# A two-layer diffusion trunk on one NeuronCore: the second head of four pairs with queries on partitions, and an issue order planned in rounds

## The chip, the core and the metric

The kernel runs on one core of a Trainium2 chip. The metric is device time in microseconds, from launch to the last result. Before the change three runs took 1436.07 us in the median (1434.85 to 1436.29). Five engines work side by side, each through its own queue in order: PE (TensorE, matmuls; its weight loads are shown as PEld), DVE (VectorE), ACT (ScalarE), POOL (GpSimd) and SP, which here issues nearly all DMAs. They wait for each other by semaphores.

## The reference, cut to what matters

Two layers act on 1024 latent tokens and 256 context tokens of width 1024. Layer A is grouped attention (16 query heads, 4 key heads, 64 wide) with normed and rotated queries and keys; layer B is neighbourhood attention on a 16 by 64 grid. Both have a SiLU gate. The part that is changed is layer A's attention over 1280 keys:

```
k_all = jnp.concatenate([kc, k], axis=1)
v_all = jnp.concatenate([vc, v], axis=1)
def block(qi):
    s = jnp.einsum('bqkgd,bskd->bkgqs', qi, k_all).astype(jnp.float32) * ATTN_SCALE
    p = jax.nn.softmax(s, axis=-1).astype(v_all.dtype)
    return jnp.einsum('bkgqs,bskd->bqkgd', p, v_all)
o = lax.map(block, qb)
yx = (o * jax.nn.silu(z)) @ w_out
```

Each layer also needs modulation vectors, `silu(c) @ w_mod + b_mod`, for a scale, a shift and a gate. The last layer's stream is normed.

## The kernel before

Matmuls are in float16, with numbers held as a high part and a low part, so that a product of two such numbers is three matmuls (high by high, high by low, low by high). Tokens are in ten tiles of 128, eight latent (`NX`) and two of context (`NC`).

**The start** (`ln_pre`, `mod_cols`, `h_kt`, `kv_mm`, `kv_post`): tokens are normed, transposed on PE (`pl`), scaled by ACT with the modulation columns (`tf`) and split; these columns come from small matmuls (`pm`, then `pmc`), one block of 128 columns at a time. Key and value projections (`pkv`) of four tiles run along, eight blocks deep.

**Layer A's attention** goes by eight pairs of heads, `u` = 0 to 7. `a_proj(u)` projects queries and gate (`pa`, line 838), norms and rotates, and lays the queries out feature-first by a DMA transpose (line 855) as `q1`, with a copy of the low part in `q2` (line 857). `mgen` then finds each query's greatest score with matmuls of their own (`pm`, line 868, and `pmc`, line 874), which DVE reduces (lines 869 and 875); `rows` turns the maxima into a row of `q2` by four small matmuls (`pr`, line 907) and one ACT write (line 908), so that the score matmul subtracts them itself. `a_att(u, pt_)` works a block of 512 queries (`pt_` 0 and 1; 2 is the context block of 256), head `i` = 0 and then 1: for each of ten key tiles it makes the scores with keys on partitions (`st`, lines 987 and 988, two PSUM banks), ACT takes the exponential twice (`ph`, line 972, and `pf`, line 974), POOL, and DVE for every sixth tile, gets the low part `pl` (lines 929 and 926), and PE multiplies weights by values, three matmuls for each 128 queries (lines 935 to 937). A constant column of the values gives the row sums. `o_out` gates, splits and transposes the result into `o_hi` and `o_lo`, two tiles for the whole layer (tags Y0 and Y1).

**Layer B's attention** (`b_att`) has queries on partitions: DVE adds the bias while it takes the maximum (line 1250), ACT exponentiates with the maximum as bias and sums (lines 1268 to 1271), one DMA transposes both parts of the weights (line 1274), and PE uses two matmuls for each tile of keys (lines 1279 and 1281).

**What sets the order.** `timeline` interleaves the generators by hand-set times; this gives a program order. `Planner` then reads the whole program as a graph, gives each instruction a cost and a latency, and runs through it once: each engine takes, of the instructions that are ready, the first in program order. Small glued groups on PE come ahead. The order it finds is fixed by added dependencies (`apply`). Modulation weights of later use are loaded during layer A by `mod_block` in blocks of 1024 by 512 (`wg`, one buffer), which wait in SP's queue among the other loads.

Of the kernel before, what the change touches and what calls it, by code (L numbers as in the profile page):

```python
# [12 lines left out]
F32 = mybir.dt.float32  # L13
F16 = mybir.dt.float16
# [7 lines left out]
P = 128  # L22
D = 1024
# [12 lines left out]
GW, GR = 64, 16  # L36
BEV, BLAG = 2, 4
# [4 lines left out]
class Planner:  # L42
# [110 lines left out]
    def graph(self):  # L153
# [58 lines left out]

        self.glued = set()
# [32 lines left out]
    def schedule(self, key=None, margin=0.0, scale=None):  # L246
        scale = scale or {}
        N = len(self.node)
        key = key or (lambda i: -1 if i in self.glued else i)
# [11 lines left out]
        free = {k: list(v) for k, v in self.free.items()}  # L261
# [12 lines left out]
        def opened(i):  # L274

            r = 0.0
            for name in self.need.get(i, ()):
# [13 lines left out]
                r = max(r, min(free[k]))  # L291
# [15 lines left out]
        while count < N:  # L307
# [29 lines left out]
            for name in self.need.get(i, ()):  # L337
                ck = self.tiles[name][0].cap_key
                free[ck].remove(min(free[ck]))
                q[ck].popleft()  # L340
# [33 lines left out]
            for name in self.users[i]:  # L374
                left[name] -= 1
                end[name] = max(end[name], fin)
                if not left[name]:
                    tl, _, _, pool = self.tiles[name]
                    free[tl.cap_key].append(end[name])
# [16 lines left out]
        self.order, self.start, self.done = order, start, done  # L396
        return max(done)

# [31 lines left out]
def trunk_kernel(ctx, tc, x, cx, cc, norm_g, b_cols, sel_c, w_mod, b_mod, a_w_in, a_qg, a_kg, a_w_out,  # L430
# [24 lines left out]
    V.tensor_copy(id16, idf)  # L455
    mhalf = main.tile([P, 8], F32, name="mhalf")
# [7 lines left out]
    s2 = main.tile([P, KT, 32], F32, name="s2")  # L464
# [41 lines left out]
    def mod_block(pool, l, c0):  # L506

        nm = f"{l}{c0}"
        wm = pool.tile([P, KT, 512], F32, name="wg" + nm, tag="wg", bufs=1)
        r, k = c0 // D, slice(c0 % D // P, c0 % D // P + 4)  # L510
        for kt in range(KT):
            DM.dma_start(wm[:, kt], w_mod[l, kt * P:(kt + 1) * P, c0:c0 + 512])
            yield 1.0
        row = pool.tile([P, P], F32, name="mrow" + nm, tag="mrow", bufs=1)
        if r == 2:
            brow = com.tile([P, 512], F32, name="brow" + nm, tag="stage", bufs=4)[0:1]
            DM.dma_start(brow, b_mod[l:l + 1, c0:c0 + 512])
        ps = ps_pj(f"pmg{nm}", shape=(P, 2, P))
        for kt in range(KT):
            for j in range(4):  # L520
                T.matmul(ps[32 * j:32 * j + 32, 0], s2[:, kt, :], wm[:, kt, j * P:(j + 1) * P], start=kt == 0,
                         stop=r < 2 and kt == KT - 1)
        if r == 2:
            for j in range(4):
                T.matmul(ps[32 * j:32 * j + 32, 0], twos, brow[:, j * P:(j + 1) * P], start=False, stop=True)
            V.tensor_scalar_mul(row, ps[:, 0], 0.5 / WS)
            for v in range(2):
                DM.dma_start(gate_d[l, v, c0 - 2 * D:c0 - 2 * D + 512].rearrange("(j c) -> j c", c=P), row[v:P:32])
        else:
            V.tensor_copy(row, ps[:, 0])  # L530
# [63 lines left out]
    xstage = [main.tile([P, 4, D], F32, name=f"xstage{j}", tag=f"Y{j}") for j in range(2)]  # L594
# [862 lines left out]
```

## Time and profile before

| what | us |
|---|---|
| median of three runs | 1436.07 |
| the profiled execution, device time | 1435.4 |
| its span, first to last instruction | 1433.3 |
| PE busy in the span | 1369.1 |
| DVE busy | 970.2 |
| ACT busy | 933.1 |
| POOL busy | 637.5 |
| PE idle from 140 to 735 us (layer A's attention) | 2.6 |
| PE idle from 870 to 1330 us (layer B's attention) | 13.3 |

Busy means that at least one instruction of the engine ran; matmuls overlap, and a matmul's listed duration is longer than the distance to the next one. The profile's views name a group by line, engine, operation and tiles (result, arrow, sources). A wait is put down to the instruction whose semaphore came last. Granted TensorE clock over the span is 0.996 of full speed.

### The profile page before, as it was taken

What the parts mean: (1) busy time and instruction counts of PE and PEld (TensorE: products, weight loads), DVE (VectorE), ACT (ScalarE), POOL (GpSimd) and SP (SyncE); (2) the same over time, 40 slices, a digit from 0 to 9 for tenths busy, and PEclk for the clock granted to TensorE, in tenths of its full rate; (3) what the DMA queues carried; (4) which work ended last, traced back from release to release, by engine and by line L of the source; (5) the groups of instructions that cost most, each with busy time, mean ns of one, the idle gap of its engine ahead of it and who ended that gap; (6) DMA issues with size and microseconds to landing.
All of it is one profiled execution on the core that took longest, in us unless ns stands there. A gap on an engine that the chain in (4) does not pass through costs nothing.

```text
span 1433.3 us, 35760 instructions
## 1 busy us (share of the span) xinstructions
PE 1369.1 (96%) x13874; PEld 951.0 (66%) x13874; DVE 970.2 (68%) x2341; ACT 933.1 (65%) x2226; POOL 637.5 (44%) x871
## 2 busy tenths in 40 slices
PE   5799999999999999999999899999999999999797
PEld 2357777777777777776555476767677676767443
DVE  4697877777777777688234736686676757686833
ACT  3452778786868786788735626776676767776811
POOL 2321677766767676677852201312222222313432
PEclk9999999999999999999999999999999999999999
DMA  9753114143222213144123405575665757567932
GB/s 282 212 149 100 40 24 115 23 122 79 59 79 59 79 43 80 34 141 120 44 89 103 148 29 111 91 157 111 136 120 108 156 95 156 92 153 142 185 102 103
DMA packets 327410, 153.01 MB, mean 107 GB/s; under 512 B 234020, under 2 KB 306372, under 8 KB 327240
## 3 DMA queue, kind: packets, MB, share of 16 engines
q1 hardware_dynamic: 326664, 150.70, 43.5%
q8 instruction: 108, 1.77, 0.5%
q14 instruction: 62, 0.51, 0.1%
q10 hardware_dynamic: 576, 0.03, 0.0%
HBM read 85.65 MB, written 12.06 MB: 68 GB/s over the span
## 4 chain that ended last, share of the span: by engine, by line
PE 84%; DVE 9%; ACT 2%; DMA 2%; issue 2%; POOL 1%; SPq 0%; DVEq 0%; POOLq 0%; ACTq 0%
PE pa L838 13%; PE pb L1167 13%; PE pvz L1199 10%; PE poa L1080 7%; PE pob L1370 5%; PE st L987 5%; PE st L988 4%; PE pm L868 3%; PE pkv L734 3%; PE pv L936 3%; PE pv L937 3%; PE pv L935 3%; PE pvz L1202 1%; PE bpv L1279 1%; DVE bk L1185 1%
## 5 line engine op out<-in xcount | busy, mean ns | idle before, releaser
L929 POOL TENSOR_TENSOR pl<-pf,ph 128x256 f16<-128x256 f32 x544 | 368.6, 704 | 134.8 <-ACT pf L974 110.5
L972 ACT ACTIVATE ph<-st 128x512 f16<-128x512 f32 x320 | 192.4, 603 | 107.3 <-PE st L988 105.7
L929 POOL TENSOR_TENSOR bph<-bpf,bph 128x256 f16<-128x256 f32 (+1 forms) x128 | 98.0, 783 | 339.4 <-ACT bpf L1270 305.9
L838 PE MATMUL pa<-wa,x 128*128 128x256 f16 x1536 | 233.6, 272 | 1.3 <-DVE q16q L664 1.3
L869 DVE TENSOR_REDUCE mxp<-pm 128x1 f32<-128x512 f32 x256 | 170.6, 684 | 49.9 <-PE pm L868 48.2
L1167 PE MATMUL pb<-hb_hi,wb 128*128 128x512 f16 (+1 forms) x640 | 194.1, 359 | 3.2 <-DVE bk L1185 3.2
L974 ACT ACTIVATE pf<-st 128x512 f32<-128x512 f32 x320 | 192.0, 604 | 1.5 <-POOL pl L929 0.5
L1199 PE MATMUL pvz<-wb,hb_hi 128*128 128x256 f16 x1024 | 172.1, 273 | 4.8 <-DVE bk L1185 3.2
L936 PE MATMUL pv<-v,ph 128*128 128x64 f16 x1280 | 162.4, 194 | 0.0
L935 PE MATMUL pv<-v,ph 128*128 128x65 f16 x1280 | 162.2, 193 | 0.0
L937 PE MATMUL pv<-v,pl 128*128 128x65 f16 x1280 | 161.1, 192 | 0.7 <-DVE pl L926 0.5
L838 PEld LDWEIGHTS <-x 128*128 128x128 f16 x1536 | 136.1, 97 | 31.8 <-DVE q16q L664 1.6
L1167 PEld LDWEIGHTS <-wb 128*128 128x128 f16 x960 | 92.4, 98 | 77.0 <-issue 3.1
L935 PEld LDWEIGHTS <-ph 128*128 128x128 f16 x1280 | 121.3, 97 | 32.3 <-issue 1.2
L1199 PE MATMUL pvz<-wb,hb_lo 128*128 128x256 f16 x512 | 139.5, 273 | 0.0
L936 PEld LDWEIGHTS <-ph 128*128 128x128 f16 x1280 | 120.5, 97 | 27.0 <-issue 0.2
L937 PEld LDWEIGHTS <-pl 128*128 128x128 f16 x1280 | 121.2, 99 | 10.3 <-DVE pl L926 1.0
L988 PE MATMUL st<-q,k 65*128 65x512 f16 x320 | 121.7, 381 | 0.0
L987 PE MATMUL st<-q,k 128*128 128x512 f16 x320 | 121.0, 379 | 0.7 <-ACT pf L974 0.5
L1199 PEld LDWEIGHTS <-hb_hi 128*128 128x128 f16 x1024 | 98.2, 98 | 27.0 <-issue 5.6
L1167 PE MATMUL pb<-hb_lo,wb 128*128 128x512 f16 (+1 forms) x320 | 114.7, 358 | 0.0
L868 PE MATMUL pm<-k,q 128*128 128x512 f16 x256 | 92.8, 379 | 2.1 <-DVE mxp L869 1.2
(244 smaller groups left out, 3263.7 us busy)
## 6 DMA issues: line engine op xcount, KB each, us to landing
wg<-in_w_mod SPq DMA_DIRECT2D x64, 256.0 KB, 3.9
wsb<-in_b_w_in SPq DMA_DIRECT2D x64, 256.0 KB, 3.0
wm<-in_w_mod SPq DMA_DIRECT2D x32, 256.0 KB, 6.1
wsa<-in_a_w_in SPq DMA_DIRECT2D x64, 128.0 KB, 2.4
xstage<-in_x SPq DMA_DIRECT2D x8, 512.0 KB, 6.7
wsoa<-in_a_w_out SPq DMA_DIRECT2D x16, 256.0 KB, 3.1
x<-in_x SPq DMA_DIRECT2D x8, 512.0 KB, 4.7
x_d<-x SPq DMA_DIRECT2D x8, 512.0 KB, 3.1
```

The costliest lines, as they stand in the source:

```text
L838: T.matmul(ps[:, :, i, :], hA(a, kt, t), wt[w][:, kt, :], start=n == 0, stop=n == 3 * KT - 1)
L869: V.tensor_reduce(mxs[i][:, t, ch:ch + 1], pm, axis=AX.X, op=ALU.max)
L929: G.tensor_tensor(lo[:, c], p32[:, c], hi[:, c], op=ALU.subtract)
L935: T.matmul(pv[:, t, :], hi[:, c], v[:, 0:65], start=first and t == 0, stop=False)
L936: T.matmul(pv[:, t, 0:HD], hi[:, c], v[:, 65:129], start=False, stop=False)
L937: T.matmul(pv[:, t, :], lo[:, c], v[:, 0:65], start=False, stop=last and t == n - 1)
L972: S.activation(ph, st, AF.Exp)
L974: S.activation(p32, st, AF.Exp)
L987: T.matmul(so, k1[:, g, kc], q1[:, :, i, :], start=True, stop=False)
L988: T.matmul(so, k2[0:65, g, kc], q2[0:65, :, i, :], start=False, stop=True)
L1167: T.matmul(ps[:, 0:n], wt[a][:, kt, which * P:(which + 1) * P], hb[b][:, kt, c0:c0 + n], start=m == 0, stop=m == 3 * KT - 1)
L1199: T.matmul(ps[:, :, j, :], hb[a][:, kt, t * P:(t + 1) * P], wt[w][:, kt, 256:512], start=m == 0, stop=m == 3 * KT - 1)
```

## The change

**The second head of pairs 0 to 3** (`QH`), query blocks 0 and 1, leaves `a_att` for a new generator `q_att`. Its scores have queries on partitions, in chunks of 512, 512 and 256 keys (`KCH`): two matmuls into a bank that row maxima use (tag mx). DVE copies them to SBUF (`qpf`, four buffers) and takes the maximum in the same instruction; the three maxima are reduced and used as ACT's bias. ACT exponentiates twice, the second time with a row sum; the split is as before; one DMA transposes high and low parts of a chunk; PE uses two matmuls for each key tile, 128 and 64 columns. Row-maximum matmuls and the maximum row of these heads fall away, and their part of `q2`'s row is set to 0 by POOL (`mgen`, `rows`, `mm`). The context block stays as it was.

**Buffers.** The weights and their transpose lie in one tile of tag Y1, which has four buffers. To make room, the output of each layer is held pair by pair, four pairs in Y0 and four in Y1 (`y_tile`, `o_dst`), the first tokens are staged tile by tile there, and the modulation weights come in half blocks (`mod_block`: two PSUM groups, the second added to the first on DVE). The condition vectors move to a pool that is closed before layer B.

**The planner** runs again five times (`refine`). Each round computes from the last schedule when PE, with its idle time taken out, would need each instruction (`deadlines`), also through buffers that one instruction frees for another (`came`); then it schedules anew, PE by its last start times and the other engines by these due times. The shortest schedule of its own model is kept.

```diff
+        before, moved = {}, set()
+        for i, x in enumerate(self.node):
+            e = self.eng[i]
+            if type(x).__name__ == "InstRegisterMove" or e in moved:
+                self.pred[i].update([before[e]] if e in before else [])
+            (moved.add if type(x).__name__ == "InstRegisterMove" else moved.discard)(e)
+            before[e] = i
...
+    def deadlines(self, margin):
+        N, start, done, cst = len(self.node), self.start, self.done, self.cst
+        due = [1e18] * N
+        idle = prev = 0.0
+        for a in self.order["PE"]:
+            idle += max(0.0, start[a] - prev)
+            prev = max(prev, start[a] + (cst[a][0] if tuple(self.node[a].tile_size or (128, 128))[1] == 128
+                                         else cst[a][0] / 4))
+            due[a] = start[a] - idle
...
+        for i in sorted(range(N), key=lambda i: -start[i]):
+            e, d = self.eng[i], done[i] - start[i]
+            for j in self.succ[i]:
+                due[i] = min(due[i], due[j] - (0.0 if self.eng[j] == e == "PE" else d + self.SEM[self.eng[j]] + margin))
+            for j in heirs.get(i, ()):
+                due[i] = min(due[i], due[j] - d - self.SEM[self.eng[j]])
...
+    def refine(self, rounds, margin, deadline):
+        best = (max(self.done), self.order)
+        self.log = [best[0]]
+        for _ in range(rounds):
+            due = self.deadlines(deadline)
+            key = [s if e == "PE" else v for s, e, v in zip(self.start, self.eng, due)]
+            best = min(best, (self.schedule(key.__getitem__, margin=margin), self.order), key=lambda b: b[0])
+            self.log.append(max(self.done))
+        self.order = best[1]
...
-        wm = pool.tile([P, KT, 512], F32, name="wg" + nm, tag="wg", bufs=1)
+        for hf in range(2):
+            wm = pool.tile([P, KT // 2, 512], F32, name=f"wg{nm}{hf}", tag="wg", bufs=1)
...
+            if not hf:
+                V.tensor_copy(row, ps[:, 0])
+            else:
+                V.tensor_tensor(row, ps[:, 0], row, op=ALU.add)
...
-    xstage = [main.tile([P, 4, D], F32, name=f"xstage{j}", tag=f"Y{j}") for j in range(2)]
+    def y_tile(shape, dt, name, j):
+        return main.tile(list(shape), dt, name=name, tag=f"Y{j}", bufs=(4, 4)[j])
+    xstage = [y_tile((P, D), F32, f"xstage{t}", t // 4) for t in range(NX)]
...
-            for i in range(2):
+            for i in ((0,) if b < NX // 2 and u in QH else (0, 1)):
...
+    def q_att(u, pt_):
...
+        for t in range(4):
+            nm = f"{u}{pt_}{t}"
+            mx = aq.tile([P, 3], F32, name="qmx" + nm, tag="qmx", bufs=2)
+            pfs = []
+            for c, (k0, n) in enumerate(KCH):
+                st = ps_mx(f"qs{nm}{c}")
+                kc = slice(k0, k0 + n)
+                T.matmul(st[:, 0:n], q1[:, t, 1, :], k1[:, g, kc], start=True, stop=False)
+                T.matmul(st[:, 0:n], q2[0:65, t, 1, :], k2[0:65, g, kc], start=False, stop=True)
+                pf = aq.tile([P, 4, P], F32, name=f"qpf{nm}{c}", tag="qpf", bufs=4)
+                pfs.append(pf)
+                V.tensor_tensor_reduce(pf.rearrange("p a b -> p (a b)")[:, 0:n], st[:, 0:n],
+                                       zero.broadcast_to([P, n]), op0=ALU.add, op1=ALU.max, scale=1.0,
+                                       scalar=-3.0e38, accum_out=mx[:, c:c + 1])
...
+            for c, (k0, n) in enumerate(KCH):
+                k = n // P
+                pq = y_tile((P, 2, 8, P), F16, f"qpp{nm}{c}", 1)
+                pp, ppt = pq[:, 0], pq[:, 1]
+                ph, pl, pf = pp[:, 0:k], pp[:, k:2 * k], pfs[c][:, 0:k]
+                S.activation(ph, pf, AF.Exp, bias=nmx)
+                S.activation(pf, pf, AF.Exp, bias=nmx, accum_out=sums[:, t, c:c + 1])
+                p_split(ph, pl, pf, 6)
+                DM.dma_start_transpose(ppt[:, 0:2 * k], pp[:, 0:2 * k].rearrange("p a b -> p (a b)"))
+                def pvs(ppt=ppt, k=k, k0=k0, t=t):
+                    for x_ in range(k):
+                        kt = k0 // P + x_
+                        vv = v1[:, kt, g, :].rearrange("p (a b) -> p a b", b=65)[:, :, 0:HD]
+                        T.matmul(pv[:, t, :].rearrange("p (a b) -> p a b", b=HD), ppt[:, x_], vv,
+                                 start=t == 0 and kt == 0, stop=False)
+                        T.matmul(pv[:, t, 0:HD], ppt[:, k + x_], v1[:, kt, g, 0:HD], start=False,
+                                 stop=t == 3 and kt == NT - 1)
+                pend.append(pvs)
+                while len(pend) > 3:
+                    pend.pop(0)()
...
         plan.schedule(margin=100.0)
+        plan.refine(5, 100.0, 300.0)
         plan.apply()
```

How the orders move is shown at three places. A row has line, operation, result, sources and the result's size; digits ahead of the underscore tell which tile of a name it is.

PE in pair 1, query block 0, before: the second head's fourth key tile (`st1103`), projection aside, and the weights-times-values triple of its first key tile:

```order
L987 LDWEIGHTS k1_115
L987 MATMUL st1103_3644<-q110_1576,k1_115 128x512
L988 LDWEIGHTS k2_116
L988 MATMUL st1103_3644<-q210_1577,k2_116 128x512
L935 LDWEIGHTS ph1100_3558
L935 MATMUL pv110_3554<-v1_117,ph1100_3558 128x65
L936 LDWEIGHTS ph1100_3558
L936 MATMUL pv110_3554<-v1_117,ph1100_3558 128x64
L937 LDWEIGHTS pl1100_3562
L937 MATMUL pv110_3554<-v1_117,pl1100_3562 128x65
```

PE in the same block now: the second head's scores of query tile 2 (`qs1020`), two projection matmuls, the first head's last key tile (`st1009`), and then the first use of a transposed chunk of query tile 0 (`qpp1000`):

```order
L1067 LDWEIGHTS q210_1555
L1067 MATMUL qs1020_3453<-k2_127,q210_1555 128x512
L914 LDWEIGHTS x00_104
L914 MATMUL pa21_3402<-wa21_2342,x00_104 128x2x128
L1140 LDWEIGHTS k1_126
L1140 MATMUL st1009_3638<-q110_1554,k1_126 128x512
L1141 LDWEIGHTS k2_127
L1141 MATMUL st1009_3638<-q210_1555,k2_127 128x512
L1091 LDWEIGHTS qpp1000_3213
L1091 MATMUL qpv10_3156<-v1_128,qpp1000_3213 128x128
L1093 LDWEIGHTS qpp1000_3213
L1093 MATMUL qpv10_3156<-v1_128,qpp1000_3213 128x64
```

The second head now runs beside the first instead of behind it, and its weights are used two query tiles after their scores.

SP from the end of pair 0 to the start of pair 1, before (`wsa` projection weights, `q1`/`q2` queries):

```order
L689 DMA wsa33_4544<-in_a_w_in 128x2x128
L855 DMA_TRANSPOSE q112_2868<-q16q14_3235 128x4x128
L689 DMA wsa40_5545<-in_a_w_in 128x2x128
L689 DMA wsa33_4544<-in_a_w_in 128x2x128
L689 DMA wsa41_5709<-in_a_w_in 128x2x128
L857 DMA q212_2869<-q112_2868 64x512
L689 DMA wsa40_5545<-in_a_w_in 128x2x128
L689 DMA wsa41_5709<-in_a_w_in 128x2x128
L689 DMA wsa42_5929<-in_a_w_in 128x2x128 x2
L855 DMA_TRANSPOSE q120_3250<-q16q20_3521 128x4x128
L857 DMA q220_3251<-q120_3250 64x512
```

SP at that place now:

```order
L933 DMA q212_2784<-q112_2783 64x512
L755 DMA wsa41_5551<-in_a_w_in 128x2x128
L755 DMA wsa33_4388<-in_a_w_in 128x2x128
L1085 DMA_TRANSPOSE qpp1000_3213<-qpp1000_3213 128x8x128
L1085 DMA_TRANSPOSE qpp1001_3229<-qpp1001_3229 128x8x128
L1085 DMA_TRANSPOSE qpp1002_3254<-qpp1002_3254 128x4x128
L755 DMA wsa40_5416<-in_a_w_in 128x2x128
L755 DMA wsa41_5551<-in_a_w_in 128x2x128
L755 DMA wsa42_5726<-in_a_w_in 128x2x128
L931 DMA_TRANSPOSE q120_3164<-q16q20_3399 128x4x128
L1085 DMA_TRANSPOSE qpp1010_3352<-qpp1010_3352 128x8x128
L1085 DMA_TRANSPOSE qpp1011_3372<-qpp1011_3372 128x8x128
```

Three transposes for each query tile now stand between the loads and the query transposes.

PE at the start, before: the modulation product of block 3 (`pmc03`), the token transposes of block 5 (`pl05`), the next modulation matmuls (`pm04`), projection:

```order
L501 MATMUL pmc03_317<-sel_82,mrow3_315 128x2 x2
L724 MATMUL pl05_481<-idf_66,xstage0_103 128x128 x4
L496 MATMUL pm04_353<-wm40_347,s2_79 32x256 x4
L496 MATMUL pm04_353<-wm41_350,s2_79 32x256 x4
L734 LDWEIGHTS x00_99
L734 MATMUL pkv0_198<-wkv0_132,x00_99 128x512
```

PE at that place now:

```order
L556 MATMUL pmc03_328<-sel_87,mrow3_326 128x2 x2
L551 MATMUL pm04_364<-wm40_358,s2_84 32x256 x4
L551 MATMUL pm04_364<-wm41_361,s2_84 32x256 x4
L556 MATMUL pmc04_375<-sel_87,mrow4_373 128x2 x2
L790 MATMUL pl05_492<-idf_66,xstage0_108 128x128
L790 MATMUL pl05_492<-idf_66,xstage1_109 128x128
```

Block 4's modulation now stands ahead of block 5's transposes.

More of the change, by code (lines that the diff above doesn't have):

```diff
@@ L36 @@
 GW, GR = 64, 16
+QH = range(0, 4)
 BEV, BLAG = 2, 4
@@ L290, in opened @@
                     return None
-                r = max(r, min(free[k]))
+                r = max(r, min(f for f, _ in free[k]))
             return r
@@ L395, in schedule @@
                     offer(j)
-        self.order, self.start, self.done = order, start, done
+        self.order, self.start, self.done, self.succ, self.came = order, start, done, succ, came
         return max(done)
+    def deadlines(self, margin):
[7 more added lines that the diff above has]
+            due[a] = start[a] - idle
+        heirs = collections.defaultdict(list)
+        for i, names in self.came.items():
+            for name in names:
+                for u in self.tiles[name][2]:
+                    heirs[u].append(i)
+        for i in sorted(range(N), key=lambda i: -start[i]):
[4 more added lines that the diff above has]
+                due[i] = min(due[i], due[j] - d - self.SEM[self.eng[j]])
+        end = max(done)
+        return [min(v, end) for v in due]
+    def refine(self, rounds, margin, deadline):
[7 more added lines that the diff above has]
+        self.order = best[1]
     def apply(self):
@@ L455, in trunk_kernel @@
     V.tensor_copy(id16, idf)
+    zero = main.tile([P, 1], F32, name="zero")
+    V.memset(zero, 0.0)
     mhalf = main.tile([P, 8], F32, name="mhalf")
@@ L829, in mm @@
                 ) + (aq.tile([P, n, P], F32, name=f"sz{u}{pt_}", tag=f"sz{pt_}", bufs=2),
-                     [aq.tile([P, 4, 3], F32, name=f"mxp{u}{pt_}{i}", tag=f"mxp{i}", bufs=3) for i in range(2)])
+                     [aq.tile([P, 4, 3], F32, name=f"mxp{u}{pt_}{i}", tag=f"mxp{i}", bufs=3) if i == 0 or pt_ == 2 or u not in QH
+                      else None for i in range(2)])
+                if pt_ < 2 and u in QH:
+                    G.memset(pairs[(u, pt_)][1][64:65, :, 1, :], 0.0)
             sz = pairs[(u, pt_)][2]
@@ L880, in rows @@
             n = PTN[pt_]
-            for i in range(2):
+            for i in ((0,) if pt_ < 2 and u in QH else (0, 1)):
                 zm = zmax[nrow[0] % len(zmax)]
@@ new lines, in q_att @@
+    def q_att(u, pt_):
+        q1, q2, sz, _ = pairs[(u, pt_)]
+        g = u // 2
+        pend = []
+        pv = psum.tile([P, 4, P], F32, name=f"qpv{u}{pt_}", tag="pv", bufs=2)
+        sums = aq.tile([P, 4, 3], F32, name=f"qsm{u}{pt_}", tag="qsm", bufs=2)
+        og = og_of(u, pt_)
+        for t in range(4):
[12 more added lines that the diff above has]
+                                       scalar=-3.0e38, accum_out=mx[:, c:c + 1])
+                yield 430 * n / 512
+            nmx = aq.tile([P, 1], F32, name="qnx" + nm, tag="qnx", bufs=2)
+            V.tensor_reduce(nmx, mx, axis=AX.X, op=ALU.max)
+            V.tensor_scalar(nmx, nmx, -1.0, CSH, op0=ALU.mult, op1=ALU.add)
+            for c, (k0, n) in enumerate(KCH):
[18 more added lines that the diff above has]
+                    pend.pop(0)()
+                yield 340 * n / 512
+        for f in pend:
+            f()
+        sm = aq.tile([P, 4], F32, name=f"qse{u}{pt_}", tag="qse", bufs=2)
+        V.tensor_reduce(sm, sums, axis=AX.X, op=ALU.add)
+        V.tensor_scalar_mul(sm, sm, 2.0 * WS * WS)
+        V.reciprocal(sm, sm)
+        oc = aq.tile([P, 4, HD], F32, name=f"qoc{u}{pt_}", tag="qoc", bufs=1)
+        S.copy(oc, pv[:, :, HD:P])
+        V.tensor_tensor(oc, pv[:, :, 0:HD], oc, op=ALU.add)
+        for t in range(4):
+            V.scalar_tensor_tensor(og[:, t, HD:P], oc[:, t], sm[:, t:t + 1], sz[:, t, HD:P], op0=ALU.mult, op1=ALU.mult)
+        og_done(u, pt_)
+        yield 500
@@ L977, in p_tiles @@
             return ph, pl
-        og = aq.tile([P, 4, P], F32, name=f"og{u}{pt_}", tag="og", bufs=2)
-        for i in range(2):
+        og = og_of(u, pt_)
+        for i in ((0,) if pt_ < 2 and u in QH else (0, 1)):
             pvs = ps_pv(f"pv{u}{i}{pt_}")
```

111 lines of the change are left out of this document (68 added, 43 removed).

## The prediction

> **What bounds the kernel now.** I read the page first (busy shares, the forty slices, the chain that ended last), then the busy times by stage, then the waits and the timeline of the stage that is changed.
>
> ```profile
> PE 1369.1 (96%) x13874; PEld 951.0 (66%) x13874; DVE 970.2 (68%) x2341; ACT 933.1 (65%) x2226; POOL 637.5 (44%) x871
> PE   5799999999999999999999899999999999999797
> PE 84%; DVE 9%; ACT 2%; DMA 2%; issue 2%; POOL 1%; SPq 0%; DVEq 0%; POOLq 0%; ACTq 0%
> ```
>
> TensorE is busy 96% of the span and carries 84% of the chain. The stage matters more than the average, so here are four stretches: the start, layer A's attention (224 to 516 us is exactly four head pairs, 73.0 us each), layer B's attention, and the end. The columns are busy us and instruction counts of PE, PEld, DVE, ACT and POOL, then clock, DMA share and GB/s.
>
> ```profile
> 0.00:140.00 140.00, 111.11 (x758) 65.72 (x759) 98.48 (x233) 56.59 (x113) 32.04 (x43) 1.00 0.67 190
> 224.00:516.00 292.00, 291.84 (x3898) 223.66 (x3897) 217.64 (x465) 224.04 (x451) 208.32 (x302) 1.00 0.28 71
> 870.00:1330.00 460.00, 446.74 (x4094) 325.92 (x4093) 326.00 (x960) 331.29 (x959) 115.99 (x157) 1.00 0.63 128
> 1330.00:1434.00 104.00, 88.56 (x521) 43.86 (x520) 51.82 (x127) 38.79 (x119) 33.11 (x35) 0.95 0.49 126
> ```
>
> In A's four pairs PE waits 0.16 us of 292: whatever leaves PE there leaves the time, as long as no other engine takes over. Per pair the others are busy 54.4 (DVE), 56.0 (ACT) and 52.1 us (POOL) of 73.0. Layer B, which already works with queries on partitions and DMA transposes, leaves PE idle 13.3 of 460 us, 2.9%. The start leaves it idle 28.9 us.
>
> **What leaves PE.** A matmul's own duration overlaps the next, so its price is the distance between starts:
>
> ```profile
> 300.05 0.27 PE L838 MATMUL pa<-wa,x 128*128 128x256 f16 x1
> 300.16 0.38 PE L987 MATMUL st<-q,k 128*128 128x512 f16 x1
> 300.38 0.38 PE L988 MATMUL st<-q,k 65*128 65x512 f16 x1
> 300.60 0.19 PE L935 MATMUL pv<-v,ph 128*128 128x65 f16 x1
> 300.63 0.19 PE L936 MATMUL pv<-v,ph 128*128 128x64 f16 x1
> 300.66 0.19 PE L937 MATMUL pv<-v,pl 128*128 128x65 f16 x1
> 300.69 0.19 PE L935 MATMUL pv<-v,ph 128*128 128x65 f16 x1
> ...
> 306.87 0.38 PE L907 MATMUL pr<-id,zmax 128*128 128x128 f16 x4
> 307.09 0.19 PE L936 MATMUL pv<-v,ph 128*128 128x64 f16 x1
> ```
>
> So 512 columns cost 0.22 us, 256 cost 0.11, 128 cost 0.055 (four in 0.22), 64 or 65 cost 0.03. The new form of the weights-times-values step stands in layer B already, ten matmuls (128 and 64 columns by turns) from 1034.25 to 1034.67, 0.084 us a pair:
>
> ```profile
> 1034.25 0.22 PE L1279 MATMUL bpv<-bv,bpht 128*128 128x128 f16 x1
> 1034.30 0.19 PE L1281 MATMUL bpv<-bv,bpht 128*128 128x64 f16 x1
> ...
> 1034.67 0.38 PE L1167 MATMUL pb<-hb_hi,wb 128*128 128x512 f16 x1
> ```
>
> The change touches eight units: the second head of four pairs, each in two blocks of 512 queries. Per unit the separate row-maximum matmuls go (4 tiles of 2x512 and 256 columns: 8x0.22 + 4x0.11 = 2.20) and the four that lay the maxima out as a row (0.22). The scores keep their columns: 20 of 512 become 16 of 512 and 8 of 256, 4.4 us both. Weights times values goes from 40 triples at 0.09 (3.6) to 40 pairs at 0.084 (3.4). That is 2.6 us a unit, and eight units make **21 us**.
>
> A rule of the Trainium skill would price the last item otherwise. TensorE: Matmul & The Clock Gate, in "LDWEIGHTS (loading the stationary operand)", gives a load the columns divided by 1.2 in ns, 107 ns for 128; were small matmuls bound by it, dropping one load in three would save 8x40x0.107 = 34 us instead of 1.6, an estimate from that page. Here three loads and three matmuls take 0.09 us together, so the loads are hidden and the rule sets no pace in this trace.
>
> **What it adds elsewhere.** ACT first, since it has least room:
>
> ```profile
> 407.15 0.62 ACT L972 ACTIVATE ph<-st 128x512 f16<-128x512 f32 x1
> 407.62 0.63 ACT L974 ACTIVATE pf<-st 128x512 f32<-128x512 f32 x1
> 1000.65 0.49 ACT L1270 ACTIVATE bpf<-bpf,bnx 128x256 f32<-128x256 f32 x1
> 1001.05 0.19 ACT L1270 ACTIVATION_READ_ACCUMULATOR bpf<-bpf,bnx 128x1 f32 x1
> ...
> 1009.16 0.60 ACT L1270 ACTIVATE bpf<-bpf,bnx 128x384 f32<-128x384 f32 x1
> 1009.66 0.19 ACT L1270 ACTIVATION_READ_ACCUMULATOR bpf<-bpf,bnx 128x1 f32 x1
> 1009.75 0.46 ACT L1271 ACTIVATE bpf<-bsc,bnx 128x256 f32<-128x256 f32 x1
> ```
>
> An exponential of 512 scores from PSUM holds ACT 0.47 us. From SBUF with a bias column it holds 0.40 for 256 and 0.50 for 384, so 0.61 for 512, and the read of the row sum 0.09. A 512 chunk then costs 0.61+0.61+0.09 = 1.31, a 256 chunk 0.89; a unit is 4x(2x1.31+0.89) = 14.0 plus 0.25 for a copy. It was 20x0.47 = 9.4 plus about 0.6 for writing the row. That is 4.2 more a unit, 8.4 a pair: ACT goes from 56.0 to 64.4 us of a pair that should last 73.0-5.2 = 67.8. It fits, at 95%. (ScalarE: Activation LUTs of the Trainium skill, under "What ACT_TABLE_LOAD costs", has 280 ns plus 0.833 an element with a bias column, less 93 of overlap: 614 ns for 512, and the sum stays as it is.)
>
> DVE trades the ten reductions of a unit against evictions that also take the maximum:
>
> ```profile
> L869 DVE TENSOR_REDUCE mxp<-pm 128x1 f32<-128x512 f32 x256 | 170.6, 684 | 49.9 <-PE pm L868 48.2
> L1250 DVE CUSTOM_DVE_ANT_0 bpf<-bsn,tb x96: 540/557/560, 832.6 to 1346.4; 128x384 f32<-128x384 f32 x96
> L1250 DVE CUSTOM_DVE_ANT_1 bpf<-bsn,tb x32: 391/425/426, 831.7 to 1349.4; 128x256 f32<-128x256 f32 x32
> ```
>
> 557 ns at 384 and 425 at 256 make 0.69 at 512, the reduction's own price, so 8x0.69+4x0.43 = 7.2 stands against 6.8; the small maxima, sums and the last scaling add 2 to 3. DVE comes to some 60 of 67.8. POOL splits the same elements in 24 pieces instead of 20 and gains about 1 us a pair. SP issues 24 more transposes a pair:
>
> ```profile
> L1274 SPq DMA_TRANSPOSE bpht<-bph x128: 1231/1347/2464, 874.4 to 1360.5; - x128
> DMA to landing us min/median/max: 3.0/3.5/4.9
> ```
>
> At 1.35 us that is 32 us of issue on SP's one queue in 67.8, beside the loads and the query transposes already there. They stand in the same queue as the loads of modulation and projection weights, and whatever waits in it holds them all. The DMA engines have room: B runs at 0.63 with about as many transposed blocks per us, A is at 0.28.
>
> All this is hidden behind PE only if the weights come back transposed in time. The new wait is TensorE's, on the transpose; behind it in PE's order stand the first head's scores and the next pair's projection, so a late one stops everything. Layer B shows the same chain: exponentials begun at 1041.78, transpose issued at 1045.52, first use at 1050.57; the second tile of the same two went out at 1049.14 and was used at 1054.46.
>
> ```profile
> 1041.78 1.01 ACT L1268 ACTIVATE bph<-bpf,bnx 128x384 f16<-128x384 f32 x2 [0.34 <-DVE bnx L1260]
> 1045.52 1.35 SPq L1274 DMA_TRANSPOSE bpht<-bph  x1
> 1049.14 1.25 SPq L1274 DMA_TRANSPOSE bpht<-bph  x1
> ...
> 1050.57 0.22 PE L1279 MATMUL bpv<-bv,bpht 128*128 128x128 f16 x1
> 1054.46 0.22 PE L1279 MATMUL bpv<-bv,bpht 128*128 128x128 f16 x1
> ```
>
> Layer B's idle share is the nearest row for what such waits cost: 2.9% of 271 us is 7.8. The lower end is A's present 0.2. I take **4 us**, the middle: B's waits for matrix evictions (the one below) have no counterpart in A, its waits for maxima do.
>
> ```profile
> PE pb L1167 <- DVE bk L1185: 3.2, 7, 0.5
> ```
>
> **What the order does elsewhere.** The rounds reorder the whole program. TensorE's order from the projection of A's last rows to the end of B is nearly what it was, so I give that nothing (between -3 and +3 by the idle of the last stretch, 15 us, of which a fifth may move). At the start it differs: the modulation product of column block 4 now stands ahead of the transposes of block 5, where it stood behind them and six projection matmuls.
>
> ```profile
> PEld pl L724 <- ACT tf L726: 13.0, 13, 1.5
> ```
>
> These 13.0 us are the transposes that wait for the scaling, which waits for those products. But the DMA share there is 0.67, and weights arriving late would only turn one wait into another. Bounds: all 13 gained, or, with loads now in another order, 5 lost; I take **-2**. The split of the modulation weights into halves leaves PE's work as it is and adds eight small additions on DVE, nothing beside 60 us.
>
> **The sum.** The profiled execution took 1435.4 us (span 1433.3), 0.7 below the median of 1436.07. 1435.4 - 21 + 4 - 2 = **1416 us**. The clock was 1.00 throughout A, so no gain is expected from it.
>
> **Rivals.** (1) *ACT sets the pace.* For: 64.4 of 67.8 us, in an order fixed beforehand, and the first head's scores share two PSUM banks that ACT empties. Against: its durations hardly vary. If it cannot be kept busier than 92%, a pair takes 70.0 and the time is 1435.4-12 = 1423 less the start; at 88% a pair takes 73.2 and all is lost: 1427 to 1437.
> (2) *The four buffers set the pace, and it is slower.* The weights and their transposes share four buffers, held from the exponential to the last use. A pair has 24 chunks, six rounds of the four, so a round may last 67.8/6 = 11.3 us, and above 73.0/6 = 12.2 the kernel loses. B's first example is 8.8+0.4 = 9.2 us, the second 12.2+0.4 = 12.6 (its exponential began at 1042.3): at that, 75.6 a pair, 4x2.6 = 10 more, 1445. For: SP's queue is half filled with transposes. Against: two exponentials a chunk here, four in B.
> (3) *The start gains all its 13 us:* 1405 and below.
> (4) *Weight loads bind after all,* by the arithmetic of the load group below (97 ns, 320 fewer, 31 us): 1387. The timeline's 0.03 us spacing speaks against it.
>
> ```profile
> L935 PEld LDWEIGHTS <-ph 128*128 128x128 f16 x1280 | 121.3, 97 | 32.3 <-issue 1.2
> ```
>
> (The page on TensorE named above is the source of that rule.)
>
> **Chances.** The forecast, 1406 to 1426, has 0.60; rival 1 0.18; rival 2 0.13; rival 3 0.08; rival 4 0.01. The range 1404 to 1438 leaves out most of 2 and 3 and all of 4, just under 2 in 10. About 0.2% (3 us) is what this kernel's measurement can tell from no change. Faster: 0.60, most of rival 1 (0.10), 3 and 4, 0.79. Same: 0.07 of rival 1. Slower: rival 2 and the rest of 1, 0.14.
>
> **What would show it.** Pairs 0 to 3 should last 67 to 69 us, pairs 4 to 7 73; row-maximum matmuls should number 192 instead of 256. PE should wait below 3% there. If ACT's gaps vanish while PE waits on its exponentials, rival 1 holds; if ACT waits for PE's use of the transposed tile, rival 2. A start that is over by more than 5 us earlier or later proves that term wrong.

## The result, and the profile after

The changed kernel takes 1412.93 us in the median of four runs (1411.77 to 1414.54), against 1436.18 for the kernel before on the same chip: a ratio of 0.9837, with a 95% interval from 0.982 to 0.9854. The forecast was 1416. The profiled execution took 1411.77 us, with a span of 1410.0. Three executions in the experiments below took far longer (2279 and 2397 us of the kernel before, 3668 us of the run without the new units) and are left out of all medians and ratios.

From the page of the changed kernel: busy times, TensorE's forty slices, and the engines' shares of the chain that ended last.

```profile
PE 1352.2 (96%) x13458; PEld 941.4 (67%) x13458; DVE 988.8 (70%) x2564; ACT 957.4 (68%) x2354; POOL 661.7 (47%) x907
PE   5899999999999999999999899999999999999897
PE 75%; DVE 8%; ACT 7%; DMA 5%; issue 2%; POOL 2%; SPq 0%; DVEq 0%; POOLq 0%; ACTq 0%
```

PE's busy time fell by 16.9 us and the span by 23.3, so some idle time went as well. PE's share of the chain is down from 84 to 75%: ACT and DMA, at 2% each before, now have 7 and 5. The same stretches of time as in the prediction (columns: busy us and count of PE, PEld, DVE, ACT, POOL, then clock, DMA share, GB/s):

```profile
0.00:140.00 140.00, 115.23 (x770) 68.71 (x771) 92.64 (x232) 60.19 (x119) 37.66 (x51) 0.98 0.66 182
224.00:516.00 292.00, 286.39 (x3698) 219.35 (x3694) 243.51 (x654) 247.29 (x558) 223.84 (x329) 1.00 0.63 125
870.00:1330.00 460.00, 448.25 (x4159) 328.65 (x4157) 342.47 (x996) 340.91 (x999) 123.41 (x165) 1.00 0.68 131
1330.00:1434.00 104.00, 72.19 (x383) 34.12 (x380) 32.10 (x69) 17.97 (x54) 25.59 (x26) 0.97 0.31 92
```

In layer A's pairs PE is now idle 5.6 of 292 us, where it was idle 0.16. These stretches hold other work than before, since everything moved forward. So the two traces are better cut at the same events: layer A's first projection matmul (`pa`), and layer B's first and last (`pb`). The timeline of PE, before:

```profile
107.47 0.60 PE L838 MATMUL pa<-wa,x 128*128 128x256 f16 x4
809.84 0.38 PE L1167 MATMUL pb<-hb_hi,wb 128*128 128x512 f16 x1
...
1296.13 0.38 PE L1167 MATMUL pb<-hb_hi,wb 128*128 128x512 f16 x1
```

And after:

```profile
105.22 0.60 PE L914 MATMUL pa<-wa,x 128*128 128x256 f16 x4
798.18 0.38 PE L1319 MATMUL pb<-hb_hi,wb 128*128 128x512 f16 x1
...
1274.88 0.38 PE L1319 MATMUL pb<-hb_hi,wb 128*128 128x512 f16 x1
```

Within a stage, the distances between the starts of PE's matmuls were added up and divided in two: what the columns need at the spacing that the trace shows (216 ns for 512, 56 for 128, 29 for 64) is called *work*, everything beyond it *waits*. Matmuls that fill only part of the array's columns count whole as work; nearly all of them are in the start and the modulation blocks.

| stage | before, us (work + waits) | after, us (work + waits) | difference |
|---|---|---|---|
| start, to A's first projection | 107.5 | 105.2 | -2.3 |
| A, to B's first projection | 702.4 (681.8 + 20.6) | 693.0 (662.9 + 30.0) | -9.4 (-18.9 + 9.4) |
| B, to its last projection | 486.3 (461.5 + 24.8) | 476.7 (461.2 + 15.5) | -9.6 (-0.3 - 9.3) |
| end | 137.2 | 135.1 | -2.1 |

Layer A gave up half of what it gained, and layer B, in which the change alters no arithmetic, gained as much as A. The forecast's total came out nearly right, and two of its four terms did not.

The waits view shows both. PE's longest waits in layer A (130 to 700 us: total, times, longest), before:

```profile
PE pm L868 <- DVE mxp L869: 1.2, 3, 0.6
PE pv L937 <- DVE pl L926: 0.5, 1, 0.5
```

After:

```profile
PE qpv L1091 <- DMA qpp<-qpp: 5.9, 8, 1.3
PE pr L983 <- DVE zmax L960: 0.8, 1, 0.8
```

And in layer B (870 to 1290 us), where PE waits nearly always for DVE to empty PSUM banks, before:

```profile
PE bsn L1230 <- DVE bmx L1250: 4.3, 8, 0.8
PE pb L1167 <- DVE bk L1185: 3.2, 7, 0.5
PE pvz L1199 <- DVE bk L1185: 3.2, 7, 0.7
PE pvz L1199 <- DVE bsz L1215: 1.1, 6, 0.2
```

After:

```profile
PE pvz L1351 <- DVE bk L1337: 3.9, 8, 0.8
PE bsn L1382 <- DVE bmx L1402: 0.4, 1, 0.4
PE bsc L1382 <- ACT bpf L1423: 0.4, 1, 0.4
PE pvz L1351 <- DVE bsz L1367: 0.2, 1, 0.2
```

Together 11.8 us before and 4.9 after. The view lists only idle time of which it knows the releaser; the table's waits hold all of it.

Two questions follow. Did the rounds of order or the new buffers speed up layer B? And what does layer A wait for? In the experiments, "A" and "B" are the table's stages in the profiled run, and ratios are to the kernel before on the same chip in the same job (its median lay between 1436.2 and 1438.3, so medians are not compared across jobs).

### The profile page after: what moved, and what is told of

Read it like the earlier page. It is cut to its first block, busy times and chain, and to the rows that moved or that the text cites. A ratio compares the mean times of both kernels' runs of the same rounds, so it can differ in the third digit from the quotient of the medians.

```text
span 1410.0 us, 35562 instructions
## 1 busy us (share of the span) xinstructions
PE 1352.2 (96%) x13458; PEld 941.4 (67%) x13458; DVE 988.8 (70%) x2564; ACT 957.4 (68%) x2354; POOL 661.7 (47%) x907
## 4 chain that ended last, share of the span: by engine, by line
PE 75%; DVE 8%; ACT 7%; DMA 5%; issue 2%; POOL 2%; SPq 0%; DVEq 0%; POOLq 0%; ACTq 0%
PE pvz L1351 12%; PE pa L914 11%; PE pb L1319 9%; PE poa L1233 7%; PE pob L1523 5%; PE st L1141 3%; PE st L1140 3%; PE pkv L800 3%; DMA qpp<-qpp 3%; PE pm L944 2%; PE pv L1012 2%; PE pv L1013 2%; PE pv L1011 2%; PE bpv L1431 1%; PE pvz L1354 1%
## 5 line engine op out<-in xcount | busy, mean ns | idle before, releaser
L1005 POOL TENSOR_TENSOR pl<-pf,ph 128x256 f16<-128x256 f32 x400 | 283.5, 731 | 72.0 <-ACT pf L1127 54.1
L1125 ACT ACTIVATE ph<-st 128x512 f16<-128x512 f32 x240 | 143.9, 602 | 64.1 <-PE st L1141 58.4
L945 DVE TENSOR_REDUCE mxp<-pm 128x1 f32<-128x512 f32 x192 | 128.6, 683 | 34.9 <-PE pm L944 34.1
L1127 ACT ACTIVATE pf<-st 128x512 f32<-128x512 f32 x240 | 144.4, 604 | 0.4
L1012 PE MATMUL pv<-v,ph 128*128 128x64 f16 x960 | 123.5, 195 | 0.0
L1011 PE MATMUL pv<-v,ph 128*128 128x65 f16 x960 | 122.7, 193 | 0.0
L1013 PE MATMUL pv<-v,pl 128*128 128x65 f16 x960 | 121.3, 192 | 0.3 <-POOL pl L1005 0.3
L1005 POOL TENSOR_TENSOR qpp<-qpf,qpp 128x256 f16<-128x256 f32 (+1 forms) x158 | 91.8, 605 | 42.7 <-ACT qpf L1083 38.1
L1011 PEld LDWEIGHTS <-ph 128*128 128x128 f16 x960 | 90.9, 97 | 21.4 <-issue 0.4
L1012 PEld LDWEIGHTS <-ph 128*128 128x128 f16 x960 | 90.5, 97 | 16.4
L1233 PE MATMUL poa<-woa,oa 128*128 128x512 f16 x384 | 92.0, 379 | 0.0
```

The costliest lines, as they stand in the source:

```text
L945: V.tensor_reduce(mxs[i][:, t, ch:ch + 1], pm, axis=AX.X, op=ALU.max)
L1005: G.tensor_tensor(lo[:, c], p32[:, c], hi[:, c], op=ALU.subtract)
L1011: T.matmul(pv[:, t, :], hi[:, c], v[:, 0:65], start=first and t == 0, stop=False)
L1012: T.matmul(pv[:, t, 0:HD], hi[:, c], v[:, 65:129], start=False, stop=False)
L1013: T.matmul(pv[:, t, :], lo[:, c], v[:, 0:65], start=False, stop=last and t == n - 1)
L1125: S.activation(ph, st, AF.Exp)
```

## Experiments: the parts of the change apart

**Without the rounds.** The order is that of the planner's first run:

```diff
         plan.schedule(margin=100.0)
-        plan.refine(5, 100.0, 300.0)
         plan.apply()
```

> The whole change, but the order is the planner's first one: the rounds are left out. Theory (the queries-on-partitions units take 20 us of matmuls out of layer A and give about 9 back in waits; layer B's 10 us and the start's 2 come from the rounds): layer B takes 486 us from its first to its last projection matmul, as before the change, rather than 477, and the time is 1423 to 1427. Rival (B gains from the per-pair output buffers and the half-size weight tiles): B stays at 477 and the time stays within 3 us of 1413.

Measured: median 1434.75 us (12 runs, 1428.15 to 1438.43), ratio 0.9979 (0.9965 to 0.9992). In the profiled execution (1431.12 us) B takes 485.5 us, as the theory said. The time missed: A is 699.5 (664.5 + 35.0). The new units took out 17 us of work, and 14 us of waits came in. Its waits in layer B, in the same window, are the old ones:

```profile
PE pvz L1351 <- DVE bk L1337: 4.1, 7, 0.7
PE pb L1319 <- DVE bk L1337: 3.2, 6, 0.7
PE pvz L1351 <- DVE bsz L1367: 1.5, 7, 0.3
PE bsn L1382 <- DVE bmx L1402: 1.0, 3, 0.4
```

So the new units alone, in the old way of ordering, are worth about 3 us.

**Without the new units.** Buffers and rounds stay:

```diff
-QH = range(0, 4)
+QH = range(0, 0)
```

> The change without the new units: no pair takes queries on partitions, the buffers and the rounds stay. Theory: layer A is as before (pairs of 73 us, TensorE idle under 1 us in four of them), layer B takes 477 us: 1424 to 1427, 10 to 12 us below before. Rival (layer B gains only because the new units shift what comes before it): no difference from before, 1434 to 1437.

Measured: median 1424.0 us of five runs, ratio 0.9901 (0.9884 to 0.9919), some 14 us below before. In the profiled execution, the shortest (1420.49 us), A is 702.6 (682.9 + 19.7), as before; B is 475.3. The theory holds: layer B does not need the new units to gain.

**The rounds alone.** The kernel before, with the new planner and its rounds, and the old buffers:

```diff
         plan.schedule(margin=100.0)
+        plan.refine(5, 100.0, 300.0)
         plan.apply()
```

The planner's other new lines, which the change's diff shows in part, go in with it.

> The kernel before with the new planner and its rounds alone, with the old output buffers and weight tiles. Theory: 1424 to 1427, like the run without the new units. Rival (per-pair output buffers): 1434 to 1437; anything between divides the gain.

Measured: median 1421.01 us, ratio 0.9881 (0.9866 to 0.9896), 17 us below before: start 104.1, A 700.5, B 478.3, end 135.4. The rival falls: the per-pair buffers are not what sped up layer B. PE's waits in layer B, in the same window, add up to 6.0 us here, against 11.8 before:

```profile
PE bsn L1278 <- DVE bmx L1298: 2.0, 5, 0.5
PE pvz L1247 <- DVE bk L1233: 1.7, 7, 0.2
PE pb L1215 <- DVE bk L1233: 1.3, 3, 0.4
PE pvz L1247 <- DVE bsz L1263: 1.0, 4, 0.2
```

The gain is a little above the range, since the start gained 3.4 us and A 1.9 too.

**Half the units.** `QH = range(0, 2)`:

> The change with the new units in two pairs instead of four. Theory, linear in the units: 10 us of matmuls less, about 5 us of waits, rounds as in the change: 1417 to 1420, halfway between the change and the run without new units. Rival (the ring of four buffers or ACT sets a pace that grows with the number of units): waits under 2 us, so 1413 to 1416.

Measured: median 1418.46 us, ratio 0.9852 (0.9834 to 0.987). A is 695.2 (672.9 + 22.4). Each two pairs remove 10 us of work. The waits do not follow in step: 19.7 without units, 22.4 with two pairs, 30.0 with four. The first two pairs shorten A by 7.4 us, the next two by 2.2. So neither expectation holds as it was put. The waits that two pairs add, 2.7 us, are nearer the rival's (under 2) than the theory's (about 5). The time is in the theory's range only because the start came out at 109.2 us here, 4 more than in the change.

## Experiments: what layer A waits for

**No round trip.** The weights-times-values matmuls of the new units read a constant tile; exponentials, splits and transposes are all still issued.

```diff
+    qcon = main.tile([P, 4, P], F16, name="qcon")
+    G.memset(qcon, 0.001)
...
-                        T.matmul(pv[:, t, :].rearrange("p (a b) -> p a b", b=HD), ppt[:, x_], vv,
+                        T.matmul(pv[:, t, :].rearrange("p (a b) -> p a b", b=HD), qcon[:, x_], vv,
...
-                        T.matmul(pv[:, t, 0:HD], ppt[:, k + x_], v1[:, kt, g, 0:HD], start=False,
+                        T.matmul(pv[:, t, 0:HD], qcon[:, x_], v1[:, kt, g, 0:HD], start=False,
```

> The change, with the new weights-times-values matmuls reading a constant tile instead of the transposed weights (the second head's result of the four pairs is left out; every exponential, split and transpose is still issued). Theory (TensorE's wait for the transposes is what A gives back): layer A, from its first projection to layer B's first, falls from 693 to 683 to 686 us and the time to 1403 to 1407. Rival (ACT and DVE with their added work set A's pace): A stays within 3 us of 693 and the time within 3 us of 1413.

Measured: median 1409.38 us, ratio 0.9803 (0.979 to 0.9816); A is 688.7 (662.7 + 26.0). This lies between the two. Of the 9.4 us of added waits the round trip holds about 4, and 5.4 stay. The run also frees each of the four buffers as soon as its transpose has landed, and no longer after PE's use of it (ACT waits 4.7 us in 130 to 443 us for such landings), so the round trip and the buffers are not told apart here. Its order, too, was planned anew, which is taken up with the larger ring below.

**The landing priced later in the plan:**

```diff
-                fin = dma + 1500
+                late = 1500 if type(x).__name__ == "InstDmaTransposeAnt" and any("qpp" in a_.bass_ap.tensor.name for a_ in x.outs) else 0
+                fin = dma + 1500 + late
```

> The change, with the planner pricing the landing of these 96 transposes 1.5 us later, so that it puts their uses later in TensorE's order. Theory (the order is set too close behind the transposes): the waits for them halve, A 688 to 690, time 1407 to 1410. Rival (the ring of four buffers): a later use holds each buffer longer, the waits move to the exponentials, A 693 or more, time 1412 to 1418.

Measured: median 1412.82 us, ratio 0.9827 (0.9811 to 0.9843); A is 693.6 (662.7 + 30.9). The wait for the transposes is gone from the waits view (130 to 700 us), and nothing is gained:

```profile
PE pmc L951 <- DMA q<-q16q: 2.8, 2, 1.6
PE st L1141 <- ACT pf L1128: 2.8, 6, 0.7
...
PE qpv L1092 <- DMA qpp<-qpp: 0.2, 1, 0.2
```

What the reader is to see: 5.9 us at one name have become 0.2, and waits of the same size stand at other names. A wait that the view names is what came last, not what the time would be without it. On A and on the time the rival's figures are right. Its ring, the four buffers that the chunks use in turn, was tried next.

**A larger ring.** The 256-key chunks get a buffer of their own, so four buffers hold six chunks' worth:

```diff
-                pq = y_tile((P, 2, 8, P), F16, f"qpp{nm}{c}", 1)
+                while len(pend) > 2:
+                    pend.pop(0)()
+                pq = (y_tile((P, 2, 8, P), F16, f"qpp{nm}{c}", 1) if c < 2 else
+                      aj.tile([P, 2, 4, P], F16, name=f"qpp{nm}{c}", tag="qps", bufs=1))
...
-                while len(pend) > 3:
-                    pend.pop(0)()
```

> The change, with the 256-key chunks in a buffer of their own, so that the ring of four holds six chunks' worth. Rival (the ring sets the pace, at a median hold of 9.5 us against a round of 12.4): A 688 or less, time 1409 or less. Theory (landing and order, not the ring): within 3 us of 1413.

Measured: median 1414.29 us, ratio 0.9833 (0.9818 to 0.9847). A is 690.0 (662.8 + 27.2), 3 us less, but the start came out at 109.3 and B at 479.2. Neither was touched: a new graph gives the planner another order everywhere. Over the kernels above, whose start differs in little or nothing, the start varies from 104.1 to 109.3 us. (Not all of this is the order: in the change's own order, in two runs below, the start took 103.3 and 105.9 us, against 105.2.) So a difference of 3 us between two kernels that were planned anew is no evidence, and this run settles nothing below that; the time did not fall.

**Both, the ring and the later landing:**

> Both of these: the larger ring and the later landing in the plan. If both matter, 1403 to 1407, near the run without the round trip; if only one does, the better of the two alone; if neither, 1413.

Measured: median 1428.35 us, ratio 0.994 (0.9924 to 0.9955), A 706.2 (662.7 + 43.5): worse than each alone, which no theory had foreseen. The waits are at the scores of both heads; why the planner's order is so bad here was not looked into.

After that, four runs kept the order of another kernel exactly, instruction by instruction on every engine, and narrowed only what one engine does. For that the planner was told the old price.

**ACT cut.** The second exponential of each new chunk works on 8 of every 128 columns:

```diff
-                S.activation(pf, pf, AF.Exp, bias=nmx, accum_out=sums[:, t, c:c + 1])
+                S.activation(pf[:, :, 0:8], pf[:, :, 0:8], AF.Tanh, bias=nmx, scale=0.0, accum_out=sums[:, t, c:c + 1])
```

> The change in exactly its own order of instructions on every engine, with the second exponential of each new chunk narrowed to 8 of every 128 columns and made a hyperbolic tangent of the bias, so that it stays finite (what the new units compute is no longer the weights). It takes some 30 us of ACT out of the four pairs. Theory (what A gives back is half the transposes' round trip and half ACT, which stands ahead of both): exponentials and so transposes are issued sooner, A falls from 693 to 686 to 689 us, time 1406 to 1410. Rival (the landing alone): A within 2 us of 693, time within 3 of 1413.

Measured: median 1412.56 us, ratio 0.9827 (0.9809 to 0.9845), A 693.2. One stretch of 313 us that covers all new units, first the change, then this run:

```profile
130.00:443.00 313.00, 305.02 (x3808) 234.90 (x3807) 263.15 (x736) 262.92 (x609) 232.82 (x348) 1.00 0.71 134
```

```profile
130.00:443.00 313.00, 304.48 (x3798) 234.33 (x3796) 263.30 (x733) 234.51 (x608) 231.84 (x347) 1.00 0.71 133
```

ACT loses 28.4 of 262.9 us, and PE gains nothing; its wait for the transposes (130 to 700 us) is 6.3 us instead of 5.9:

```profile
PE qpv L1091 <- DMA qpp<-qpp: 6.3, 7, 1.3
```

ACT, 84% busy, is not what holds the chain, and the theory's half falls. What the transposes themselves wait for in SP's queue is shown by the waits view of that queue (140 to 443 us), in the change:

```profile
SPq L1085 <- POOL pl L1005: 40.1, 42, 4.7
SPq L1085 <- POOL qpp L1005: 24.0, 16, 3.9
```

POOL's splits (`pl` those of the first heads, `qpp` those of the new units) are what mostly comes last there; with ACT cut the two rows are still 28.3 and 23.5 us. No run shortened POOL's work, so POOL (232.8 of 313 us busy) is a rival that stays untested.

**DVE cut.** The row maxima run over 32 of 512 keys, for every head that still has them: the first heads of pairs 0 to 3 and both heads of pairs 4 to 7. Those heads' exponentials are hyperbolic tangents (not shown):

```diff
-                            V.tensor_reduce(mxs[i][:, t, ch:ch + 1], pm, axis=AX.X, op=ALU.max)
+                            V.tensor_reduce(mxs[i][:, t, ch:ch + 1], pm[:, 0:32], axis=AX.X, op=ALU.max)
```

> The change in exactly its own order on every engine, with the row maxima of the first heads taken over 32 of 512 keys (and their exponentials made hyperbolic tangents, to stay finite): some 90 us of DVE less in layer A, 0.5 us at each of 192 reductions. Theory (ACT and the transposes): A within 3 us of 693, time within 4 us of 1413. Rival (DVE, 83% busy in those pairs, is what holds the chain back): A 687 or less, time 1407 or less.

Measured: median 1409.43 us, ratio 0.9813 (0.9791 to 0.9834), A 689.8 (663.2 + 26.6). The groups of that line, in the change and in this run:

```profile
L945 DVE TENSOR_REDUCE mxp<-pm 128x1 f32<-128x512 f32 x192 | 128.6, 683 | 34.9 <-PE pm L944 34.1
```

```profile
L945 DVE TENSOR_REDUCE mxp<-pm 128x1 f32<-128x32 f32 x192 | 35.7, 188 | 65.1 <-PE pm L944 62.2 <-PE pv L1013 1.1
```

Two thirds of these reductions belong to pairs 4 to 7. In the stretch with the new units DVE loses 36.8 of 263.2 us, and PE is idle 6.4 us instead of 8.0:

```profile
130.00:443.00 313.00, 306.61 (x3846) 236.09 (x3845) 226.31 (x742) 267.11 (x618) 235.69 (x352) 1.00 0.74 138
```

93 us less of DVE go with an A that is 3.2 us shorter in the profiled execution, less than either reading needs. The theory's range for A is missed by 0.2, the rival's by 2.8. By the times alone the effect is not shown: the interval of the ratio overlaps that of the change. Layer B, which the cut does not touch, came out 1.0 us longer and the start 1.9 shorter, so single executions in one order differ by this much.

**No round trip and ACT cut,** in the order of the run without the round trip:

> The run without the round trip, in exactly its order, with the same narrowing of the second exponentials. Theory (the 5 us of A's added waits that stayed without the round trip are ACT's): A falls from 689 to 683 to 685, time 1402 to 1405. Rival (they come from the order, or from DVE): A within 2 us of 689, time within 3 us of 1409.

Measured: median 1409.28 us, ratio 0.9803 (0.9784 to 0.9821), A 687.7 (662.9 + 24.7). The rival holds: 1.0 us, and the time is the same.

**No round trip and DVE cut,** likewise in that order:

> The run without the round trip, in exactly its order on every engine, with the row maxima of the first heads taken over 32 of 512 keys as in the run with DVE cut (and hyperbolic tangents for the first heads' exponentials, to stay finite). Theory now (the waits that stayed without the round trip are for the two shared score banks, which DVE empties): A falls from 689 to 683 to 686 us, by at least what the same cut gave with the round trip (3 us), time 1403 to 1406. Rival (they come from the order alone, or from POOL): A within 1.5 us of 689, time within 3 us of 1409.

Measured: median 1406.73 us, ratio 0.9789 (0.9765 to 0.9813), A 686.7 (662.7 + 23.9). DVE's cut is worth 2.0 us of A here, below the theory and above the rival; again the intervals of the ratios overlap, and B came out 1.6 longer. With no round trip and little DVE, 3.3 of the 9.4 us of added waits remain.

No run that leaves the kernel's result as it is beat the change by more than the measurement can tell.

## Why the prediction was right, and where its steps were not

The sum was 1435.4 - 21 + 4 - 2 = 1416. By the stages it is 1435.4 - 18.9 (A's work) + 9.4 (A's waits) - 2.3 (start) - 9.6 (B) - 2.1 (end) = 1411.9, against 1411.77 in the profiled run. That the total came out close is luck: too much taken off for the work (2.1 us) and too little added for waits (5.4) stand against a gain in B and at the end (11.7) for which nothing was put down.

- **The work removed, 21 us:** right. 18.9 us left layer A, 20.0 against the run without the new units, and two pairs alone gave 10.0. Were small matmuls bound by their weight loads at the rate that the Trainium skill states (TensorE: Matmul & The Clock Gate, "LDWEIGHTS (loading the stationary operand)"), the 320 loads that fell away would have saved 34 us in place of 1.6, an estimate from that page. The trace shows otherwise: 18.9 us of work in all leaves no room for that, nor for the 31 us of rival 4, which is out.
- **The waits in A, +4 us, bounds 0.2 to 7.8:** mis-sized. The bounds were in the profile's own idle time of PE. By that measure the waits are 8.0 of 313 us over 130 to 443 us (2.6%, under the 3% forecast) against 1.7 before: 6.3 more, inside the bounds and above the 4. By matmul starts they are 9.4; but by starts layer B's share would have been 24.8 of 486.3 (5.1%), and the upper bound some 13.8. So it is the middle that failed, not the bounds. Which waits B's share stands for was not asked: in B, before the change, PE's matmuls waited 0.2 us for the transposed weights and nearly all the rest for DVE, whereas A's longest wait, 5.9 us, is for the transposes, and the next, for a maximum, is 0.8.
- **"TensorE's order from the projection of A's last rows to the end of B is nearly what it was, so I give that nothing (between -3 and +3)":** wrong. B and the end gained 11.7 us. PE's order did hardly change; what the rounds reorder is the other engines, and PE's waits were for these. Counted in the traces of layer B, by operation and result, as the longest sequence that two traces share: before and with the rounds alone, 4096 of 4159 matmuls keep their order, and only 720 of DVE's 936 instructions. The row for it was quoted (PE waiting for DVE at the key projections), and it was used only to argue that such waits have no counterpart in A. The rounds alone give 17 us by the medians, 15.1 between the profiled executions, 9.8 of these in B and the end.
- **The start, -2 us:** right by its number, -2.3, but not more than starts scatter: 104.1 to 109.3 us over the replanned kernels, 103.3 to 105.9 in the change's own order. The waits of the transposes for the scaling halved, from 13.0 us to

```profile
PEld pl L790 <- ACT tf L792: 6.7, 7, 1.5
```

and only 2.3 of these 6.3 us came out as time. The step supposed that late weights would take the rest; that was not followed up.
- **Rival 1, ACT's pace:** excluded, in the change's own order, by the run that cut 28 us of ACT. Forecast at 95% of a pair, ACT was busy 183.5 of the 211 us from 205 to 416 (pairs 1 to 3), 87%.
- **Rival 2, the four buffers:** not shown. The eight units ran from the first exponential at 144.2 us to the last use at 441.6, 24 rounds of 12.4 us. That is above the 12.2 from which the prediction said the kernel would lose, and it gained. The step behind it, that a pair cannot end before its new unit, was wrong: the units trail behind, and pair 4's first scores stand at 416.1. The larger ring did not lower the time. The sign that the prediction named, ACT waiting for PE's use of a transposed tile, is there but small: 5.1 us in the 313.
- **Rival 3, all 13 us at the start:** did not happen.
- **Pairs of 67 to 69 us, then 73:** cannot be read so. First scores of pairs 1 to 5 stand at 204.9, 273.9, 346.1, 416.1 and 497.8: distances of 69.0, 72.2, 70.0, and 81.7 where the trailing units are finished. The row-maximum matmuls number 192, as forecast.

What the two parts are worth depends on each other. The rounds bring 14 us without the new units (0.9901 with the new buffers; 0.9881, 17 us, with the old ones, and the intervals overlap), and about 20 with them (0.9979 to 0.9837). The units bring 3 us without the rounds and 9 with them. Of the 9.4 us of waits in A, the runs place about 4 at the round trip of the transposes, in a kernel planned anew. DVE's share is uncertain. From A's first projection to the first score of pair 5, by which the new units are finished, its cut takes off 2.7 us with the round trip (392.6 to 389.9) and 0.3 without (386.3 to 386.0); what it gains behind that lies in pairs whose row maxima stood in the kernel before. So some 3 to 5 us stay open. They may come from the order, since replanned starts scatter by as much, or from POOL; neither is shown. Which of DVE's instructions the rounds moved to help layer B was not isolated either.

## What to carry to other kernels

Cut both traces at the same events and compare stage by stage, even when the total is as forecast: two wrong terms can cancel. When a change brings a new way of ordering along, run that part alone, and look at the engines that PE waits for, since PE's own order can stay the same while its waits go. To find out whether a busy engine is a bound, shorten its work in an unchanged order; here 28 us of an engine that was 84% busy were worth nothing.

## What the runs showed of the hardware that was not expected

The DMA engines' share over the new units rose from 0.25 to 0.71: the row of 130 to 443 us above, against the same stretch of the kernel before (the last three columns are clock, DMA share and GB/s):

```profile
130.00:443.00 313.00, 311.30 (x4050) 236.47 (x4049) 239.20 (x507) 230.60 (x466) 212.09 (x307) 1.00 0.25 64
```

The transposes take long to issue, as they did in layer B, and land unevenly. The view of the tile `qpp` in the changed kernel has a median issue of 1.25 us (durations in ns, minimum, median, maximum), and a landing between 2.4 and 5.8 us after the issue began, for the 27 of 96 of which the trace can tell it:

```profile
L1085 SPq DMA_TRANSPOSE qpp<-qpp x96: 1188/1247/2507, 147.6 to 436.4; - x96
DMA to landing us min/median/max: 2.4/3.4/5.8
```

One late transpose, from the timeline of SP and then of PE. Two issues go out back to back, and PE stands 1.32 us for one of them.

```profile
427.17 2.61 SPq L1085 DMA_TRANSPOSE qpp<-qpp  x2
```

```profile
430.96 0.38 PE L944 MATMUL pm<-k,q 128*128 128x512 f16 x1
432.67 0.23 PE L1091 MATMUL qpv<-v,qpp 128*128 128x128 f16 x1 [1.32 <-DMA qpp<-qpp]
```

At the start, the matmuls were not all granted the full clock. The stretch from 20 to 40 us, the change and then the kernel before with the rounds alone (the kernel before had 1.00 there):

```profile
20.00:40.00 20.00, 18.05 (x120) 9.01 (x123) 7.37 (x18) 2.79 (x6) 0.00 (x0) 0.91 0.77 212
```

```profile
20.00:40.00 20.00, 18.24 (x122) 9.70 (x115) 9.69 (x25) 5.86 (x10) 0.33 (x1) 0.76 0.95 272
```

By an estimate from these rows, 18.05 us at 0.91 and 18.24 at 0.76, the lower clock cost 1.6 and 4.4 us at most, and the start was still shorter in both than before. It is not a matter of the order alone: the run with DVE cut has the change's order, and a clock of 1.00 in that stretch:

```profile
20.00:40.00 20.00, 17.29 (x132) 9.00 (x132) 8.38 (x22) 4.13 (x7) 0.00 (x0) 1.00 0.81 223
```

What lowered the clock was not tried.
